# Row-wise softmax on one core: two first blocks of 5 and 11 rows in place of three of 3, 5 and 8

## The chip, the cores and the metric

One core of a Trainium2 chip runs the kernel. The metric is the device time of one execution in microseconds (us). The profile's span is 1.8 us shorter than this time.

## The reference

The input is 16 x 1024 rows of 512 float32 numbers, 33.55 MB; the output has the same size.

```python
x_max = np.max(x, axis=-1, keepdims=True)
exp_x = np.exp(x - x_max)
return (exp_x / np.sum(exp_x, axis=-1, keepdims=True)).astype(np.float32)
```

## The kernel before

The rows are cut into blocks. A block (R, s) has R rows for each of the 128 partitions (the lanes of the on-chip memory) and lives at row s of a buffer of 96 rows; everything is computed in place. VectorE (DVE) takes the maximum of a group of about 8 rows, ScalarE (ACT) does the exponentials row by row with their sums, DVE takes the reciprocal and scales row by row. All loads are issued from SyncE (SP), all stores from ACT, so that there are two DMA queues. A transfer is said to land when its completion is signalled. The last two blocks reuse rows 0 to 31 and wait for the stores from there. (Cut from the kernel; "..." marks what is left out.)

```python
CHUNKS = [
    (3, 0), (5, 3), (8, 8), (16, 16), (16, 32), (16, 48), (16, 64), (16, 80), (16, 0), (16, 16),
]
EARLY = 8                            # loads issued ahead of everything
AFTER_STORE = {2: [8], 3: [9]}       # loads that reuse rows
FINISH_BEFORE = (1, 2, 3)            # scale what is open before these blocks' first maximum
STORE_ROWS = {3: 8, 4: 8, 5: 8}      # store these blocks in halves
...
    for k, (R, _) in enumerate(CHUNKS):
        m = max(1, round(R / GROUP))              # groups in a block, GROUP = 8
        cuts = [R * i // m for i in range(m + 1)]
...
        for g, (k, a, _, _) in enumerate(groups):
            if waiting is not None and a == 0 and k in FINISH_BEFORE:
                scale(waiting)                    # reciprocal, scaling, store
                waiting = None
            rowmax(g)
            exps(g)
            if waiting is not None:
                scale(waiting)
            waiting = g
```

## Time and profile before

| | before |
|---|---|
| time, median of the first 3 runs | 161.54 us (161.52 to 162.06) |
| span | 159.7 us |
| DVE / ACT busy | 78% / 58% of the span |
| moved by DMA | 67.13 MB, 420 GB/s over the span |
| first full block's maximum begins | 32.37 us |
| last store is issued / lands | 144.77 / 158.86 us |

The page has two candidates for the bound: the DMA engines, which are full in every slice but the first and the last, and DVE, which carries 70% of the chain that ended last. A window of the trace counts a DMA packet in the stretch where it begins, so a short stretch can show more than 1.00.

### The profile page before, as it was taken

How to read it: one execution, taken by the hardware profiler on the slowest of the kernel's cores; microseconds unless marked ns; L12 is line 12 of the kernel's file. 1: busy time of each engine (PE TensorE's matmuls, PEld its weight loads, DVE VectorE, ACT ScalarE, POOL GpSimd, SP SyncE). 2: the span in 40 equal slices, each digit the busy share in tenths (PEclk: the TensorE clock that was granted, in tenths of full speed). 3: DMA queues.
4: the chain of work that ended last, by engine and by line, in shares of the span. 5: the costliest groups of instructions: out<-in, count | busy, mean ns of one | idle time of the engine just before them, and what ended most of it. 6: DMA issues, size and time to landing. Idle time of an engine off the chain costs nothing.

```text
span 159.7 us, 521 instructions
## 1 busy us (share of the span) xinstructions
DVE 123.9 (78%) x162; ACT 93.3 (58%) x257; POOL 0.2 (0%) x4
## 2 busy tenths in 40 slices
DVE  0481870799699999999999999999999999762000
ACT  0718129208994959595868677686859595930000
POOL 0000000000000000000000000000000000000000
DMA  7999999899999999999999999999999999999993
GB/s 269 433 464 411 389 447 446 383 412 466 402 441 431 460 435 396 439 418 468 427 414 439 414 484 427 396 447 402 435 439 476 418 402 468 443 402 468 427 410 164
DMA packets 3315, 67.13 MB, mean 420 GB/s; under 512 B 368, under 2 KB 368, under 8 KB 624
## 3 DMA queue, kind: packets, MB, share of 16 engines
q1 hardware_dynamic: 1440, 33.56, 49.5%
q10 hardware_dynamic: 1872, 33.56, 48.9%
q14 instruction: 3, 0.02, 0.0%
HBM read 33.55 MB, written 33.55 MB: 420 GB/s over the span
## 4 chain that ended last, share of the span: by engine, by line
DVE 70%; ACT 14%; issue 3%; DMA 3%; DVEq 0%; ACTq 0%
DVE shift L101 38%; DVE held L123 30%; ACT held L109 14%; DMA held<-in_x_dram 3%; DVE recip L121 2%; DVEq L175 0%; ACTq L109 0%
## 5 line engine op out<-in xcount | busy, mean ns | idle before, releaser
L109 ACT ACTIVATE held<-held,shift 128x512 f32<-128x512 f32 x128 | 90.5, 709 | 43.4 <-DVE shift L101 33.2
L101 DVE TENSOR_REDUCE shift<-held 128x8 f32<-128x4096 f32 (+2 forms) x17 | 70.6, 4161 | 4.5 <-DMA held<-in_x_dram 4.5
L123 DVE TENSOR_SCALAR held<-held,recip 128x512 f32<-128x512 f32 x128 | 52.2, 481 | 0.6
L109 ACT ACTIVATION_READ_ACCUMULATOR held<-held,shift 128x1 f32 x128 | 24.0, 187 | 0.0
L121 DVE RECIPROCAL recip<-sums 128x8 f32<-128x8 f32 (+2 forms) x17 | 3.3, 193 | 15.8 <-ACT held L109 15.8
L109 ACT ACT_TABLE_LOAD x1 | 1.3, 1283 | 4.5 <-DMA held<-in_x_dram 4.5
L164 POOL MEMSET const-bfloat16-1.0<- 128x1 bf16 x1 | 0.1, 102 | 0.0
L164 POOL MEMSET const-uint8-127<- 128x1 uint8 x1 | 0.1, 102 | 0.0
L164 POOL MEMSET const-float32-1.0<- 128x1 f32 x1 | 0.1, 99 | 0.0
L164 POOL MEMSET const-float32-0.0<- 128x1 f32 x1 | 0.1, 98 | 0.2 <-issue 0.2
## 6 DMA issues: line engine op xcount, KB each, us to landing
held<-in_x_dram SPq DMA_DIRECT2D x7, 4096.0 KB, 41.8
out_dram<-held ACTq DMA_DIRECT2D x4, 4096.0 KB, 21.0
out_dram<-held ACTq DMA_DIRECT2D x7, 2048.0 KB, 35.5
held<-in_x_dram SPq DMA_DIRECT2D x1, 2048.0 KB, 11.3
held<-in_x_dram SPq DMA_DIRECT2D x1, 1280.0 KB, 6.7
out_dram<-held ACTq DMA_DIRECT2D x1, 1280.0 KB, 20.0
held<-in_x_dram SPq DMA_DIRECT2D x1, 768.0 KB, 4.5
out_dram<-held ACTq DMA_DIRECT2D x1, 768.0 KB, 15.7
```

What stands on the lines that cost most here:

```text
L101: nc.vector.reduce_max(out=shift[g], in_=place[k][:, a:b, :], axis=AX, negate=True)
L109: nc.scalar.activation(out=place[k][:, r, :], in_=place[k][:, r, :], func=EXP, bias=shift[g][:, r - a : r - a + 1], scale=1.0, accum_out=s ...
L121: nc.vector.reciprocal(out=recip, in_=sums[g])
L123: nc.vector.tensor_scalar_mul(out=place[k][:, r, :], in0=place[k][:, r, :], scalar1=recip[:, r - a : r - a + 1],)
L164: nc = _bacc.Bacc("TRN2", target_bir_lowering=False, num_devices=1)
```

## The change

The first three blocks become two. The second one is computed in two groups, of 5 and 6 rows, and each group is stored as soon as it is scaled. The intent: fewer rounds in which DVE and ACT wait for each other before the full blocks begin.

```diff
-    (3, 0), (5, 3), (8, 8), (16, 16), (16, 32), (16, 48), (16, 64), (16, 80), (16, 0), (16, 16),
+    (5, 0), (11, 5), (16, 16), (16, 32), (16, 48), (16, 64), (16, 80), (16, 0), (16, 16),
 ]
-EARLY = 8
-AFTER_STORE = {2: [8], 3: [9]}
+EARLY = 7
+AFTER_STORE = {1: [7], 2: [8]}
-FINISH_BEFORE = (1, 2, 3)
+FINISH_BEFORE = (1, 2)
-STORE_ROWS = {3: 8, 4: 8, 5: 8}
+STORE_ROWS = {1: 5, 2: 8, 3: 8, 4: 8}
...
-        m = max(1, round(R / GROUP))
+        m = -(-R // GROUP)
```

## The prediction

> **What bounds it now.** I read four views, in this order. First the page: do all engines have slack, and does the DMA?
>
> ```profile
> DVE 123.9 (78%) x162; ACT 93.3 (58%) x257; POOL 0.2 (0%) x4
> ...
> DMA  7999999899999999999999999999999999999993
> ...
> HBM read 33.55 MB, written 33.55 MB: 420 GB/s over the span
> ...
> DVE 70%; ACT 14%; issue 3%; DMA 3%; DVEq 0%; ACTq 0%
> ```
>
> The span is 159.7 us (161.54 us by the clock outside it, so 1.8 us are not in the profile). The DMA row has a 9 or an 8 in every slice but the first and the last. The last line is the chain that ended last, and it seems to say the opposite: 70% of the span on DVE. But its shares sum to 90%, and in order of time the chain stops at 144.74 us, 15 us before the end. So the second view is the stretches by time (us, DVE, ACT and POOL busy, clock, DMA share, GB/s):
>
> ```profile
> 1.00:2.00 1.00, 0.00 (x0) 0.00 (x0) 0.00 (x0) 1.00 0.98 289
> 2.00:3.00 1.00, 0.00 (x0) 0.00 (x0) 0.00 (x0) 1.00 0.94 362
> 3.00:15.00 12.00, 5.94 (x6) 5.73 (x14) 0.00 (x0) 1.00 1.04 429
> 15.00:60.00 45.00, 36.08 (x44) 26.13 (x73) 0.00 (x0) 1.00 1.00 429
> 60.00:108.00 48.00, 47.79 (x65) 36.13 (x102) 0.00 (x0) 1.00 1.00 431
> 108.00:157.00 49.00, 34.09 (x49) 25.29 (x72) 0.00 (x0) 1.00 1.01 433
> ```
>
> Whatever DVE does (half idle in the third row, never idle in the fifth), the DMA engines are full and move 429 to 433 GB/s. Nothing moves before 1.05 us, and the last data packet ends at 157.5 us; the rest to 159.7 us is the last landing (158.86) and the closing barrier. 67.11 MB over those 156.5 us are 429 GB/s. **The bound is the DMA engines, from the first packet to the last.**
>
> Third, how near DVE is to being a second bound. The last store (4 MB), seen alone:
>
> ```profile
> L129 ACTq DMA_DIRECT2D out_dram<-held x1: 339/339/339, 144.8 to 144.8; - x1
> DMA to landing us min/median/max: 14.1/14.1/14.1
> ```
>
> The three stores that are issued at 115.6, 131.1 and 144.8 land at 139.55, 149.21 and 158.86, one each 9.66 us: that is 4.19 MB at 434 GB/s, back to back. The store before the last one lands at 149.21; taking the 1.4 us that lie between the last packet and its landing, its data end near 147.8. The last store is issued at 144.77 and could move its first byte about 1.1 us later (as the first load does), at 145.9. So DVE's work comes about 1.9 us before the DMA would run dry. A DVE delayed by more would show; a DVE that is earlier would not.
>
> Fourth, the chain of waits in order of time, for the beginning that the change rewrites (start us, us, what):
>
> ```profile
> 0.00 4.46 DMA held<-in_x_dram
> ...
> 4.48 1.76 DVE shift L101
> ...
> 10.01 2.74 DVE shift L101
> ...
> 12.78 3.64 ACT held L109 x10
> ...
> 16.66 2.07 DVE held L123 x5
> 18.73 4.34 DVE shift L101
> ...
> 23.10 5.75 ACT held L109 x16
> ...
> 29.11 3.26 DVE held L123 x8
> 32.37 4.34 DVE shift L101
> ```
>
> Three rounds of maximum, exponentials and scaling run strictly one after the other here, because each early block is finished before the next one's maximum begins; at 32.37 us the first 16-row block starts.
>
> **What the skill says.** "DMA: Bandwidth & Descriptors", Specifications, gives 435 GB/s as the fabric ceiling of the 16 engines; the trace has 429 to 433, so there is little above it. "HBM Reference", Specifications (TRN2), gives some 358 GB/s per core, but says a core alone streams at about 425: this trace agrees with the second. The DMA page, Queues, rings and completion order, says each engine takes turns between its queue rows packet by packet. I use this to share the rate: with 32 KB load packets against 16 KB store packets, stores should get a third, 0.144 MB/us or 14.5 us for 2.10 MB; the trace's stores land at 38.74, 53.36, 67.95 and 82.45, each 14.5 us, which agrees. "Perfetto Trace Analysis", What "DMA-bound" means, asks which DMA resource binds; here neither issuing queue is full (a load takes 0.33 us to issue), so it is the engines.
>
> **The change part by part.** *Bytes.* The same 67.11 MB. One load fewer, whose 16 completion packets of 9 ns are nothing. *Packets.* One packet per partition and transfer. The duration by size in the trace's store packets is 234 ns (6 KB), 385 (10 KB), 611 (16 KB). 128 of each over 16 engines: 1.87+3.08+4.89 = 9.84 us before. Stores of 5, 5 and 6 rows: 3.08+3.08+3.7 (12 KB, estimated at 38.4 ns per KB) = 9.86. The same. Loads: 6 KB packets took 281 ns on average, as the queue's start-up falls in them (289 and 362 GB/s above); 5 and 11 rows in place of 3, 5, 8 save perhaps 0.1 us of the 10.35 us that these took. Sum for the bound: **0 to -0.2 us, I take -0.1**.
>
> *DVE and ACT.* The first 16 rows, by the durations of the chain (a row costs 0.70 us on ACT, 0.40 on DVE's scaling, 0.53 on DVE's maximum). The first load of 5 rows: 3 rows landed at 4.46, 8 rows at 7.50, thus 0.431 MB/us, and 0.52 MB more land at 5.7. Maximum 2.8: 8.5. Five rows on ACT 3.64: 12.2. Reciprocal 0.2, scaling 2.07: 14.5, first store (before: 10.04). Maxima of 5 and 6 rows 2.74+3.27: 20.5. ACT meanwhile does 5 rows from 17.2 to 20.9 and goes straight on with 6 rows to 25.2; DVE scales the 5 rows by 23.2 (second store) and, when ACT is done, the 6 rows in 0.2+2.5: 27.9 (third store). The first full block's maximum starts at 27.9 in place of 32.37: **DVE is 4.5 us earlier**, since two rounds that didn't overlap became two that partly do. From there the order of instructions is unchanged (the order of the built program shows the same rows), so the last store would be issued near 140.3 in place of 144.77.
>
> *Is that worth something?* No: the last store then waits some 6.4 us in the queue instead of 1.9. All 4.5 us lie beside DMA work that is full anyway.
>
> *Does the DMA go hungry early?* The first store comes 4.4 us later, but the load queue then has 5+11+16+16+16 rows, or 16.8 MB, issued without any wait, some 39 us of work. So loads fill the gap.
>
> **Rivals.** *(1) DVE is the bound, as the chain's 70% suggests.* Then 4.5 us come off: 157.0 us, faster by 2.8%. Against it: the DMA is full in each stretch. Only idle DMA time could be recovered, and I find none.
>
> *(2) New waits on completion semaphores.* Eight semaphores are shared by 22 transfers, and the built program shows other pairings: the seventh load now waits for the first store's landing, and some half-block stores wait for the landing of earlier ones. Small store packets get a small share: 10 of 42 KB, 0.103 MB/us, so the first two stores (1.31 MB each) take 12.7 us each from 15.7, and the third (12 of 44 KB) 13.3: their data end at 28.4, 41.1, 54.4, landings about 1.5 us later. The load that reuses these rows goes out near 56 in place of 53.44, while two earlier loads are still queued (the like ones landed at 66.13 and 80.66): hidden. The first half of the first full block is stored next; at 14.5 us for 2.10 MB it lands near 70.5. The first half of the third full block wants to be stored at 72.5 (76.96 less 4.5) and shares its semaphore: 2 us to spare. If that is missed, ACT and DVE stall by a few us, which the 6.4 us above absorb. Time if it bites: still about 161.5; only if waits exceed 6 us would it be slower.
>
> *(3) Loads too late for an earlier DVE.* Full blocks landed at 24.29, 37.14, 51.58, 66.13, 80.66, 95.22, 109.93; DVE wants them at 27.9, 41.5, 56.9, 72.4, 87.8, 103.3, 118.7. At least 3.6 us remain, and loads come earlier rather than later, since the stores start later. A wait here would cap the DVE's lead, not cost time.
>
> **Range.** 161.54 - 0.1 gives 161.4 us. The runs of before scatter from 161.52 to 162.06, upwards only; the packets' start may give 0.3 more or nothing. So 160.9 to 162.1. Faster than 2% needs 158.3 us, which is below what 67.11 MB take at 433 GB/s (155.0 us) plus 1.05 before the first packet, 2.2 after the last and 1.8 outside (160.0): 2%. Slower by 2% needs 3.3 us of idle DMA: 1%. Within: 97%.
>
> **What would show it.** Right: the DMA row still full and some 430 GB/s in each stretch; first full block's maximum near 27.9; the last store issued near 140.3 but taking near 18.5 us to land, not 14.1; the last landing near 158.8. Wrong: a stretch well below 429 GB/s (then a queue ran dry, and the issue whose wait ended there tells why); a rate above 433 in the first 30 us, where loads run with fewer stores beside them (then the mix of reads and writes matters, which I take not to); or DVE ending no earlier, idle in front of a semaphore.

## The result

The changed kernel takes 161.78 us (median of 6, 161.65 to 161.92), the kernel before 161.56 us in the same rounds (median of 6, 161.52 to 162.06). Ratios here are the mean time of one kernel's fast runs over that of the other's of the same rounds, so not quite the ratio of the medians: 1.0009, 95% interval 0.9996 to 1.0022. **The time is the same** by the verdict's 2%. All the same, five of the six runs of the kernel before (161.52 to 161.58) lie below all six of the changed one; this 0.2 us is taken up under "The first load's size".

The page of the changed kernel, for the lines shown of before:

```profile
DVE 123.9 (77%) x162; ACT 93.2 (58%) x257; POOL 0.2 (0%) x4
...
DMA  6999998999999999999999999899999999999993
...
DVE 69%; ACT 14%; DMA 3%; issue 1%; DVEq 0%; ACTq 0%
```

The span is 160.0 us. Nothing on this page tells that anything happened; the chain of waits even looks as before. The chain in order of time (start us, us, what) shows the beginning:

```profile
0.00 5.41 DMA held<-in_x_dram
...
14.25 2.74 DVE shift L101
...
17.01 7.87 ACT held L109 x22
...
25.13 2.46 DVE held L123 x6
27.60 4.34 DVE shift L101
```

The 11 rows go through ACT in one unbroken run of 7.87 us, because the maximum of the 6 rows is ready before ACT has done the 5. The first full block's maximum begins at 27.6 us, 4.8 us earlier than the 32.37 of before. That lead is kept to the end; the last store, alone:

```profile
L129 ACTq DMA_DIRECT2D out_dram<-held x1: 338/338/338, 140.0 to 140.0; - x1
DMA to landing us min/median/max: 19.1/19.1/19.1
```

It is issued 4.8 us earlier and takes 5.0 us longer to land (19.1 us in place of 14.1): it lands at 159.06 us, where before it was 158.86. The stretches of time (us, DVE, ACT and POOL busy, clock, DMA share, GB/s) show why:

```profile
1.00:2.00 1.00, 0.00 (x0) 0.00 (x0) 0.00 (x0) 1.00 0.66 143
3.00:15.00 12.00, 5.83 (x8) 4.91 (x11) 0.00 (x0) 1.00 1.01 432
15.00:60.00 45.00, 40.96 (x47) 30.75 (x86) 0.00 (x0) 1.00 1.01 426
60.00:108.00 48.00, 47.75 (x64) 35.02 (x97) 0.00 (x0) 1.00 1.00 432
108.00:157.00 49.00, 29.34 (x47) 22.48 (x64) 0.00 (x0) 1.00 1.01 436
```

DVE does 40.96 us of work from 15 to 60 us where it did 36.08, and 29.34 us after 108 us where it did 34.09. From 3 to 157 us DMA is full in every stretch in both kernels. The work moved; the bound did not. (Whether the engines themselves, the memory or the path between them sets these 430 GB/s, no run here tells; "DMA" below stands for all of it.)

### The profile page after: what moved, and what is told of

It reads as the page before. It is cut to its first block, busy times and chain, and to the rows that moved or that the text cites. A ratio compares the mean times of both kernels' runs of the same rounds, so it can differ in the third digit from the quotient of the medians.

```text
span 160.0 us, 513 instructions
## 1 busy us (share of the span) xinstructions
DVE 123.9 (77%) x162; ACT 93.2 (58%) x257; POOL 0.2 (0%) x4
## 4 chain that ended last, share of the span: by engine, by line
DVE 69%; ACT 14%; DMA 3%; issue 1%; DVEq 0%; ACTq 0%
DVE shift L101 39%; DVE held L123 29%; ACT held L109 14%; DMA held<-in_x_dram 3%; DVE recip L121 1%; DVEq L175 0%; ACTq L109 0%
```

## The experiments

Three theories stood at first. **A**: the DMA engines bound both kernels, and DVE is a close second bound, closer before than after. **B**: DVE bounds, as the chain's 70% says. **C**: DMA bounds and DVE is far from it in both. Taking DMA work away, or giving DVE more, tells them apart.

### Less DMA work

One store of 2.10 MB, or both stores of one block (4.19 MB), are left out in mid-run in either kernel. The results are wrong; loads and arithmetic stay.

```diff
-        if since is not None:
+        if since is not None and not (k == 5 and b == 8):   # c1; c2: k == 4 and b == 8
+        if since is not None and not (k == 5):              # c3; c4: k == 4
```

> The kernel before, with one 2.10 MB store left out in mid-run (wrong result on purpose). Theory A (the DMA engines bound both kernels, and DVE is only 1.9 us from being the bound before): 2.10 MB at 434 GB/s are 4.84 us of DMA work, but only the first 1.9 us of it can come off before DVE binds: 159.7 us. Theory B (DVE bounds, DMA is merely busy): no change, 161.5 us. Theory C (DMA bounds alone, DVE is far from it): 156.7 us.

> The changed kernel with the same 2.10 MB store left out. Theory A: the spare of DVE is 6.9 us here (the data of the store before the last end near 148.0, the last store could begin at 141.1), more than the 4.84 us of work taken away, so all of it comes off: 156.9 us. Theory B: no change, 161.8 us. So A has this kernel 2.8 us ahead of the same cut of the kernel before, B has them equal.

> The kernel before, with the two stores of one block (4.19 MB) left out. Theory A: DVE binds already after 1.9 us, so no more comes off than with one store left out: 159.7 us. Theory B: 161.5 us. Theory C: 151.9 us.

> The changed kernel with the two stores of the same block (4.19 MB, 9.7 us of DMA work) left out. Theory A: 6.9 us come off and then DVE binds: 154.9 us, 4.8 us below the same cut of the kernel before, which is the lead of DVE that the change brings and that is hidden at full bytes. Theory B: 161.8 us. Theory C: 152.1 us.

| | kernel before | changed kernel |
|---|---|---|
| all stores (from the main comparison) | 161.56 us | 161.78 us |
| 2.10 MB less | 158.58 us (c1) | 157.10 us (c2) |
| 4.19 MB less | 158.70 us (c3) | 154.11 us (c4) |

The kernel before had 161.60 us in the rounds of c1 to c4 (7 runs, 161.51 to 162.43); the changed kernel was not run in them. Against it c2 and c4 are faster (ratios 0.9705 and 0.9522). c1 and c3 (0.9797, interval 0.9769 to 0.9825, and 0.9804, 0.9770 to 0.9838) are clear of no change.

B falls: time goes down when DMA work does, though DVE does exactly what it did. C falls too: the kernel before gains 3.0 us from the first cut and nothing from the second. A has the pattern right, and its sizes too small: I had expected 1.9 us before DVE binds. The last store of c1, then the stretch ahead of its first packet:

```profile
L129 ACTq DMA_DIRECT2D out_dram<-held x1: 338/338/338, 144.8 to 144.8; - x1
DMA to landing us min/median/max: 11.1/11.1/11.1
```

```profile
143.00:145.50 2.50, 1.75 (x5) 0.00 (x0) 0.00 (x0) 1.00 0.03 13
```

Here the DMA engines have run dry (13 GB/s) while DVE still scales, so the store meets empty queues. From issue to landing it takes 11.1 us; c3, c4 and d1 below, where the queues are empty as well, give 11.1 each. That of c4:

```profile
L129 ACTq DMA_DIRECT2D out_dram<-held x1: 339/339/339, 140.3 to 140.3; - x1
DMA to landing us min/median/max: 11.1/11.1/11.1
```

That is the number with which a spare is to be read off: issue to landing in the full kernel less 11.1 (for a last store of this size, 4.19 MB). It gives 14.1 - 11.1 = **3.0 us** before and 19.1 - 11.1 = **8.0 us** after. With it the four fit (c1 by construction, since the 11.1 were first read there; the other three are tests): c1 and c3 161.56 - 3.0 = 158.6; c2 161.78 less the whole 4.84 us = 156.9 (157.10 measured); c4 161.78 - 8.0 = 153.8, plus 0.3 since its last store was issued at 140.3 rather than 140.0, is 154.1. Between c3 and c4 lie 4.6 us: that is the change's gain, in the time at last, once DMA is no longer in the way.

### More DVE work

With all bytes and a right result: one maximum in mid-run is taken twice, which makes DVE 4.33 us later from there.

```diff
             rowmax(g)
+            if (k, a) == (6, 0):        # changed kernel: (5, 0), the same block
+                for _ in range(1):
+                    rowmax(g)
             exps(g)
```

> The kernel before with one row maximum of a block in mid-run done twice: DVE is 4.33 us later from there on, bytes and result unchanged. Theory A (DMA bounds, DVE 1.9 us from it): 161.55 + 4.33 - 1.9 = 164.0 us. Theory B (DVE bounds): 165.9 us. Theory C (DVE far from it): 161.5 us.

> The changed kernel with the same 4.33 us of extra DVE work. Theory A: the spare is 6.9 us, so nothing shows: 161.8 us. Theory B: 166.1 us.

d1 took 162.81 us (162.76 to 163.27), d2 161.90 us (161.79 to 162.01). They were run on another chip. The kernel before itself scattered on this chip (median 162.24, from 161.54 to 163.18), and against it both are "the same" (ratios 1.0043, interval 1.0007 to 1.0079, and 0.9982, 0.9942 to 1.0023), so I read the profiles beside the times: spans 161.0 and 160.0 us, where the undelayed kernels had 159.7 and 160.0. The last store of d1 is issued at 149.0 us and takes 11.1 us to land, as in c1. That of d2:

```profile
L129 ACTq DMA_DIRECT2D out_dram<-held x1: 339/339/339, 144.3 to 144.3; - x1
DMA to landing us min/median/max: 14.8/14.8/14.8
```

In d1 the delay eats the 3.0 us and 1.3 us are left over (4.33 - 3.0), which is the growth of the span. In d2 the store is 4.3 us later than in the changed kernel and lands at 159.09, as without the delay (159.06): nothing left over. B, which had both kernels 4.33 us slower, is refuted a second time. I had expected 164.0 for d1, again from a spare of 1.9.

### No small first blocks at all

```diff
-    (5, 0), (11, 5), (16, 16), ...
+    (16, 0), (16, 16), ...              # EARLY = 6, AFTER_STORE = {0: [6], 1: [7]}
-FINISH_BEFORE = (1, 2)
+FINISH_BEFORE = ()
-STORE_ROWS = {1: 5, 2: 8, 3: 8, 4: 8}
+STORE_ROWS = {0: 8, 1: 8, 2: 8, 3: 8}
```

> No small first block at all: eight blocks of 16 rows, the first one loaded whole, half-block stores in the first four. DVE starts near 12.4 us in place of 4.5, but with no block finished ahead of the next one its end should come near 143, 4.8 us ahead of need. Theory A: small first blocks are worth nothing to the time as long as DVE's last scaling comes before 147.8; 161.8 us, with what the head of a 32 KB first load adds (theory H: up to 0.3 us). Theory B (DVE bounds): its end follows DVE.

162.14 us (161.99 to 162.21), where the kernel before had 161.59 on that chip; ratio 1.0016, interval 0.9982 to 1.0050. DVE starts only at 12.4 us, and yet the last store is issued at 140.4 us, as early as in the changed kernel, since with FINISH_BEFORE empty no round is run alone (ACT's share of the chain that ended last is 7%, where it was 14%). So what the small first blocks buy is some 0.5 us by medians, and at most 0.8 us by the interval, though they bring DVE's start from 12.4 to 4.5 us. f4 differs in several settings at once, and where its 0.5 us come from was not looked into.

### The first load's size

By medians the changed kernel is 0.2 us slower, and its first stretch (143 GB/s from 1 to 2 us, where it was 289) suggests the first load. d3 and f3 are one kernel, the one before with only its first two blocks swapped; d4 is the changed kernel with 3 and 13 rows.

```diff
-    (3, 0), (5, 3), (8, 8), ...         # before
+    (5, 0), (3, 5), (8, 8), ...         # d3 and f3
-    (5, 0), (11, 5), ...                # changed
+    (3, 0), (13, 3), ...                # d4, STORE_ROWS = {1: 6, ...}
```

> The kernel before with its first two blocks swapped (5, 3, 8 rows in place of 3, 5, 8), nothing else. In the changed kernel's trace the DMA engines' summed busy time is 0.27 us behind by 3 us from the start and stays so to the end: ten of the 16 engines begin their first packet at 1.63 us or later, where before all had begun by 1.43. Theory H (the size of the first load's rows sets this head): this kernel shows the same late start and runs in 161.75 us. Theory N (the 0.2 us come from the later part, or are chance): it runs in 161.55 us.

> The changed kernel with first blocks of 3 and 13 rows in place of 5 and 11 (13 computed as 6 and 7). Theory H: the head is that of the kernel before (all engines begun by 1.45 us), so 161.55 us. Theory N: 161.8 us.

> The kernel before with the first loads of 5, 3 and 8 rows once more, as its timing was unclear on a chip where the kernel before itself scattered from 161.5 to 163.2. Theory H (the size of the first load's rows sets the head of the DMA work): summed busy time by 3 us near 1.65 where the 3-row heads have 1.76 to 1.83, and 0.15 us longer than the kernel before. Theory N: no difference.

The head of the DMA work does go with the first load: from 1 to 3 us the 3-row kernels moved 326 (before), 347 (d4) and 341 GB/s (d1), the 5-row ones 287 (changed), 266 (d3) and 282 (f3). But the times do not follow. d3 took 161.65 us and f3 161.67 us, against 161.59 us for the kernel before in f3's rounds (ratio 0.9987, interval 0.9956 to 1.0018); d4 took 162.18 us, from 161.71 to 162.92, in place of the 161.55 expected; but the kernel before had 162.24 in the same rounds (ratio 1.0002, interval 0.9967 to 1.0037), so d4 decides nothing. In its profiled run (162.92 us) two stray packets end at 159.57 and 159.74 us where half the engines are done by 158.0. By the packet records of that run only 12 to 14 of the 16 engines had a packet during most of the time from 3.0 to 4.8 us; from 3 to 9 us that is 0.32 us of all engines lost, where the kernel before lost 0.02 and the changed one less than 0.01. That the engines which stood idle there are the two that end late is likely, but not shown. So neither theory is settled: a later head is there, 0.2 us in the time is not shown to come from it, and the scatter of the other runs above 162 us stays unexplained.

### Larger store packets: a try for a faster kernel

```diff
-STORE_ROWS = {3: 8, 4: 8, 5: 8}
+STORE_ROWS = {}                        # f1; f2: the changed kernel with {1: 5}
```

> The kernel before with every 16-row block stored whole, so 32 KB packets in place of pairs of 16 KB. In the trace two 16 KB store packets take 1222 ns and one of 32 KB takes 1213: over 128 partitions and 16 engines that is 0.07 us for each of three blocks. Theory A (the DMA engines' summed work sets the time): 0.2 us off, 161.35 us where the kernel before has 161.55. Rival (the early stores now come later and the reuse of their rows holds up loads): 162 us or more.

> The changed kernel with every 16-row block stored whole. Theory A: 0.2 us off the 161.78 us of the changed kernel, 161.55. Rival, as for the run ahead of this: no gain or a loss.

f1 took 162.00 us (161.71 to 164.06), f2 161.79 us (161.66 to 161.98), the kernel before 161.59. Neither is faster than its parent (the changed kernel, f2's parent, was not run on that chip); no version that I ran beats both kernels. The profile of f1 teaches most, though it is of a slow execution (163.43 us; four of the six lie from 161.71 to 162.08). The two queues (packets, MB, share of 16 engines) from 80 to 108 us, first in the kernel before, then in f1; q1 are the loads, q10 the stores:

```profile
q1 hardware_dynamic: 268, 8.16, 67.5%
q10 hardware_dynamic: 268, 3.87, 32.3%
```

```profile
q10 hardware_dynamic: 212, 6.42, 53.1%
q1 hardware_dynamic: 207, 5.77, 47.8%
```

In both, the two queues send about equally many packets (of data, without the completions that the lines count too: 249 loads and 236 stores, then 176 and 196). With 16 KB store packets against 32 KB load packets the loads get two thirds of the engines; with 32 KB against 32 KB they get half. So the half-block stores hold the stores back in favour of the loads. In f1 the last load lands at 127.85 us in place of 109.93. That its rows came free later, the rival put on record, is not the reason: it was issued at 76.93 us, where before it was 82.53. (So too in f2: issued at 77.73 and landed at 124.01, in the changed kernel 87.63 and 107.70.) DVE waits for it and for the one before (f1, in order of time; idle time before and what ended it in brackets):

```profile
108.52 4.42 DVE L101 TENSOR_REDUCE shift<-held 128x8 f32<-128x4096 f32 x1 [0.75 <-DMA held<-in_x_dram]
...
127.88 4.42 DVE L101 TENSOR_REDUCE shift<-held 128x8 f32<-128x4096 f32 x1 [3.80 <-DMA held<-in_x_dram]
```

These 4.6 us are more than the 3.0 us of spare; in this profiled run the DMA engines then run dry near 148 us, and the last store, issued at 149.43, again takes 11.2 us to land. Why other executions of f1 lost less is not shown. f2, in its profile, loses as much to late loads (5.4 us of DVE waits after the first one) and still keeps its time: the lead that the change brings is what pays. Its last store has 13.4 us to landing, 2.3 us of spare.

## Why the prediction was right

**The bound.** Predicted: DMA, with no idle time to recover, so 161.4 us and "same". Right; shown by c1 and c2, where 2.10 MB less take off 3.0 and 4.7 us with DVE's work unchanged, and by c3, where the next 2.10 MB take off nothing once DVE binds.

**DVE's lead.** Predicted 4.5 us, with the full block's maximum at 27.9 and the last store at 140.3. Measured 4.8 us, 27.6 and 140.0. The difference began with the first load, which landed at 5.41 and not at 5.7.

**That the lead is worth nothing.** Right: 18.5 us to landing predicted, 19.1 measured, in place of 14.1. d2 shows it from the other side.

**The spare.** This term of the argument was mis-sized: 1.9 us before and 6.4 us after, where the runs give 3.0 and 8.0. The step that failed is "the last data packet ends at 157.5 us" and with it the 1.4 us from last packet to landing. I had read the end of the packets off stretches that count a packet where it begins; by the packet records the last one ended at 158.53 us, 0.3 us before the landing. The start, too, was too long: with empty queues the first packet of c1's last store began 0.84 us after its issue, where I had 1.1. With both put right the sum gives 3.3 us; the last 0.3 is that this store needs 9.9 us from first packet to last on empty queues, where stores back to back come every 9.66. The verdict did not hang on it, but the expectations of c1, c3, c4 and d1 did, and each was off by 0.8 to 1.2 us.

**The packets.** Predicted -0.1 us; measured +0.2 us by medians. The interval of the ratio (0.9996 to 1.0022, so -0.1 to +0.4 us) includes no difference; the predicted -0.1 lies at its edge. The summed packet time did fall by 0.1 us (157.42 to 157.33 us over 16 engines), but the time is not that sum.

**The rivals.** (1) DVE as the bound: refuted by c1 to c4, d1 and d2. (2) Waits on shared semaphores (the counters that signal a landing): one of them did bite. I had the first half-store of the first full block land near 70.5 with 2 us to spare; it landed at 72.97, since the early stores were slower than I had worked out (the first landed at 31.64 and not near 29.9, the third at 58.43 and not near 55.9), and the store that shares its semaphore went out at 73.05, 0.9 us after its scaling was done. DVE was not idle for it, and the 8.0 us of spare would have covered it. (3) Loads too late: no wait after the first load in the changed kernel. f1 and f2 show that this rival is real as soon as store packets grow.

## What to carry to other kernels

Here a chain of waits on a compute engine (70% of the span) was not the bound; it ended 14 us before the last landing. In such a case look at how long the last transfer takes from issue to landing, and compare it with the same transfer on empty queues; the difference is what the compute engine may be late. Work moved off a second bound showed in the time only when the first one was relieved (4.6 us between c3 and c4, nothing gained at full bytes), and one run that relieves it on purpose, even with a wrong result, says at once how much lies hidden. Where the two queues shared the DMA engines here, packet sizes went with who got how much, and in f1's profile, where store packets were larger, late loads went with a last landing 1.7 us later (160.60 in place of 158.86); a saving of 0.2 us had been expected.

## What the Trainium skill lacked or had wrong

- "DMA: Bandwidth & Descriptors", Queues, rings and completion order, says that an engine changes queues at packets, but not what follows for shares: at equal packet counts (268 and 268) 32 KB load packets took 67.5% of the engines and 16 KB store packets 32.3%; at 32 KB each it was 47.8% for the loads and 53.1% for the stores.
- The same page, Specifications, lists about 358 GB/s per core as HBM's limit; this core, alone, moved 429 to 433 GB/s in each long stretch of the kernel before. The row is not wrong but needs its explanation, which "HBM Reference", Specifications (TRN2), gives: it is the share of a core when both of a pair run, and a core alone streams at about 425.
- The same page, Latency and other measured facts, gives about 600 ns to the first byte for this kind of queue. Here 0.84 us passed from the issue's start to the first packet with empty queues; the issue itself is 0.34 us of that, and the page does not say from where it counts. A 4.19 MB store on empty queues took 11.1 us from issue to landing in each of four runs; the page has a formula for the whole of a transfer only for those issued from GpSimd, none for this kind of queue, and that number is what one needs to read a spare.
- No page says what these runs show of a first load of 5 rows (10 KB packets): the engines filled later than with one of 3 rows (6 KB), 266 to 287 GB/s in place of 326 to 347 from 1 to 3 us. Its worth in time was not settled.
